# Attention output and state input of a hybrid decoder step as pairs of 64-column matmuls, and the weight sums spread anew

## The chip, the cores and the metric

The kernel runs on one core of a Trainium2 chip. The metric is the device time of one launch in microseconds, the median of the runs. A core has TensorE (PE, matmuls, its weight loads are listed as PEld), VectorE (DVE), ScalarE (ACT), GpSimd (POOL), and SyncE (SP), which here issues most DMAs.

## The reference

One decoder layer over 2064 prompt tokens (16 learned ones and 2048) and 8 x 4 sample tokens, model width 1024, FP32. A combined input projection feeds an attention group (8 heads of 64, 2 key/value heads, window of 128) and a state-space group (32 groups of 16 channels, 64 complex states each). Both outputs are normalised and projected together, and an MLP with squared ReLU follows. Cut to what the change touches:

```python
# attention of one block of 128 tokens: kk, vv are the block before and the block itself
logits = jnp.einsum('bnqkgd,bnskd->bnkgqs', qb, kk) * (HEAD_DIM ** -0.5)
p = sink_softmax(logits, mask, sink)
o = jnp.einsum('bnkgqs,bnskd->bnqkgd', p, vv)            # attention output
# state-space input of a group
bu_re = jnp.einsum('bsgh,gph->bsgp', ug, bbar_re)        # state input
bu_im = jnp.einsum('bsgh,gph->bsgp', ug, bbar_im)
# MLP
a = jnp.square(jax.nn.relu(jnp.einsum('bsd,df->bsf', hn, w_up)))
y = jnp.einsum('bsf,fd->bsd', a, w_down)
```

## The kernel before

The program runs in four stages. `phase_u` (to some 158 us) projects the state-space channels and prepares their matrices. `phase_att` (to 510 us) is the attention loop. `phase_mix` (to some 802 us) does the GLU of the state-space group and the output projection. `phase_mlp` does the MLP by a scheme of seven products in place of eight for 2 x 2 blocks, which needs sums and differences of blocks of the weights.

**The loop.** `tile_step(i)` handles one tile of 128 tokens and, beside it, one pair of state-space groups `pr = i + 1`. The order on TensorE, VectorE, ScalarE and GpSimd is that of the code for the first fifteen steps (`manual_schedule`); the last two steps and the other stages are ordered by a scheduler. In a step TensorE does the scores of heads (`scores`, L820), the q, k, v of the tile after next (`qkv`, L439 and L440), the transposes of the last tile's second half of probabilities (`ptrans`, L861), the second scores, the transposes of q and k (`tr`, L790 and L792), the state output (`s_out`, L942 and L946), the attention output of the last tile (`pv`, L873), the next state input (`s_in`, L908), and the transposes of this tile's first half of probabilities (L861 again). The probabilities of that half are scaled by VectorE on L852 (`normal`), the others by ScalarE on L854.

`pv` puts two heads on the two halves of 128 output partitions. The stationary tile `vr` holds 64 columns of v between zeros (192 columns), and a slice of 128 columns puts v left or right, so that four matmuls add up in one bank, of which two add zeros to each half. `s_in` does the same with `wz`, 64 columns of one group left and of the other right, with zeros between. `vr` and `wz` are filled with zeros once by GpSimd, and `s_load` loads `wz` by two DMAs a pair of groups. `s_out` uses the two row halves of the array instead: its stationary and moving slices are of 64 partitions each (L946). The two-bank pool `b2` holds one buffer, which `s_out`, `s_in` and the transposes of the projection share; `mm` has six banks.

**The weight sums.** `weight_sums` loads a block of 128 x 4 x 256 weights, does four subtractions (L1508, L1511, L1512, L1513) and stores the block. There are 64 blocks (32 for `w_up`, 32 for `w_down`). `sums_step` advances those under way and begins a new one, if the count is below `last`. Two steps a tile run in the loop on GpSimd (30 blocks), three a tile in the projection on VectorE up to block `SLAST = 44` (14 blocks), and one at every fourth step of the MLP's first product phase on VectorE (20 blocks). The store of a block waits in SP's queue for its sums.

**The projection.** For each tile `squares` adds squares on GpSimd (L1209, L1211), TensorE sums them over partitions (`norm_of`, L1216), VectorE scales (L1217) and GpSimd takes the power (L1218), which the evacuations of the projection's banks need (L1235 on ScalarE, L1340 on VectorE). `post_a` and `post_b` use GpSimd's power on L157. `turn` transposes the result two tiles later (L1363).

## Time and profile before

| | us |
|---|---|
| median of 3 runs (2098.76 to 2102.39) | 2098.87 |
| profiled execution | 2100.17 |
| its span, first to last instruction | 2098.4 |
| TensorE busy | 2037.1 (97%) |
| VectorE busy | 1591.9 (76%) |
| ScalarE busy | 1292.0 (62%) |
| GpSimd busy | 347.7 (17%) |
| share of the chain that ended last: TensorE | 82% |

Busy time is the sum of an engine's instructions. Matmuls are pipelined, so the start of the next line, not the end of a matmul, shows what a group takes. In the chain of waits each piece of time is put down to what the last instruction, followed back, waited for. A granted clock of 1.00 is 2.4 GHz on TensorE, 0.5 is 1.2 GHz. Spans on GpSimd are rough.

### The profile page before, as it was taken

To read this page: it belongs to the slowest core of one execution; us is meant where nothing else is said; L and a number is where in the kernel's file an instruction comes from. 1 tells how busy PE (TensorE), PEld (TensorE's weight loads), DVE (VectorE), ACT (ScalarE), POOL (GpSimd) and SP (SyncE) were. 2 spreads that over 40 slices of the span, in tenths; PEclk is the share of its full clock that TensorE was granted. 3 is DMA by queue.
4 is the path that set the end of the run, shared out by engine and by line. 5 is a ranking of instruction groups with operands and counts; after the bars stand their busy time and mean duration, and the time that the engine had idled before them with its cause. 6 is when DMAs were issued, how large, how long until landed. Compare 5 with 4: busy or idle time off the path is not lost.

```text
span 2098.4 us, 36246 instructions
## 1 busy us (share of the span) xinstructions
PE 2037.1 (97%) x12652; PEld 1915.3 (91%) x12652; DVE 1591.9 (76%) x3302; ACT 1292.0 (62%) x2787; POOL 347.7 (17%) x372
## 2 busy tenths in 40 slices
PE   7899999997999999999999999999999999999997
PEld 7877888876788879999999999999999999999996
DVE  8957888785867665898967866878668758787686
ACT  6644666666756556588655554886555547875555
POOL 5602444452424440000000000000000000000001
PEclk9999999998999999999999999999999999999999
DMA  8897778775686367888444655554445554444454
GB/s 297 239 212 211 195 201 203 203 183 137 212 270 212 118 203 231 277 276 281 143 143 136 194 184 140 164 167 138 136 141 186 172 152 136 154 142 140 136 164 147
DMA packets 360671, 387.10 MB, mean 184 GB/s; under 512 B 105208, under 2 KB 250264, under 8 KB 360472
## 3 DMA queue, kind: packets, MB, share of 16 engines
q1 hardware_dynamic: 293800, 378.14, 59.1%
q10 hardware_dynamic: 65792, 4.20, 2.2%
q0 software_dynamic: 896, 2.46, 0.4%
q8 instruction: 99, 1.62, 0.3%
q14 instruction: 84, 0.69, 0.1%
HBM read 303.26 MB, written 82.46 MB: 184 GB/s over the span
## 4 chain that ended last, share of the span: by engine, by line
PE 82%; DVE 7%; DMA 5%; ACT 2%; issue 2%; POOL 1%; SPq 1%; ACTq 0%; POOLq 0%; DVEq 0%
PE mm L111 22%; PE mm L112 22%; PE mm L113 22%; PE mm L439 4%; PE mm L873 2%; PE mm L440 2%; PE mm L820 1%; PE b L908 1%; PE mm L861 1%; DMA xr<-in_xT_dram 1%; PE b L946 1%; DVE U L1530 1%; PE b L1604 1%; PE b L942 1%; DMA UD<-U 1%
## 5 line engine op out<-in xcount | busy, mean ns | idle before, releaser
L111 PE MATMUL mm<-vh,wsh 128*128 128x352 f32 (+1 forms) x2624 | 838.2, 320 | 1.7 <-ACT wsh L96 1.7
L112 PE MATMUL mm<-vl,wsh 128*128 128x352 f32 (+1 forms) x2624 | 838.5, 320 | 0.0
L113 PE MATMUL mm<-vh,wsl 128*128 128x352 f32 (+1 forms) x2624 | 814.4, 320 | 0.0
L96 ACT ACTIVATE wsh<-wr 128x512 fp32r<-128x512 f32 x684 | 430.6, 630 | 440.9 <-PE mm L112 427.4
L97 DVE TENSOR_TENSOR wsl<-wr,wsh 128x512 fp32r<-128x512 f32 x684 | 472.4, 691 | 200.7 <-ACT wsh L96 198.5
L111 PEld LDWEIGHTS mm<-vh,wsh 128*128 128x128 f32 x2624 | 493.8, 188 | 2.2 <-ACT wsh L96 2.0
L112 PEld LDWEIGHTS mm<-vl,wsh 128*128 128x128 f32 x2624 | 493.1, 188 | 0.0
L113 PEld LDWEIGHTS mm<-vh,wsl 128*128 128x128 f32 x2624 | 488.0, 188 | 0.0
L157 POOL TENSOR_TENSOR yst<-yst,nhalf 128x1 f32<-128x1 f32 (+2 forms) x15 | 12.4, 826 | 1235.1 <-DVE yst L156 876.0
L1530 DVE TENSOR_TENSOR U<-U,mm 128x352 f32<-128x352 f32 (+3 forms) x240 | 140.1, 584 | 77.6 <-PE mm L113 76.9
L97 DVE TENSOR_TENSOR vl<-U,vh 128x352 fp32r<-128x352 f32 (+3 forms) x348 | 175.6, 506 | 1.5 <-ACT vh L96 1.0
L96 ACT ACTIVATE vh<-U 128x352 fp32r<-128x352 f32 (+3 forms) x348 | 162.9, 470 | 6.4 <-PE mm L112 6.2
L1563 ACT ACTIVATE U<-U 128x352 f32<-128x352 f32 (+1 forms) x192 | 92.6, 483 | 9.6 <-DVE U L1530 5.6
L1564 ACT ACTIVATE U<-U 128x352 f32<-128x352 f32 (+1 forms) x192 | 93.7, 489 | 4.2
L111 PE MATMUL mm<-xh,uwh 128*128 128x264 f32 (+1 forms) x256 | 73.3, 297 | 12.9 <-DVE U L531 7.0
L439 PE MATMUL mm<-qw,axh 128*128 128x512 f32 x224 | 85.0, 404 | 0.0
L112 PE MATMUL mm<-xl,uwh 128*128 128x264 f32 (+1 forms) x256 | 75.0, 296 | 0.0
L840 ACT ACTIVATE e<-e,mx 128x256 f32<-128x256 f32 x128 | 63.4, 497 | 16.5 <-DVE mx L834 16.5
L113 PE MATMUL mm<-xh,uwl 128*128 128x264 f32 (+1 forms) x256 | 72.9, 294 | 0.0
L863 ACT ACTIVATE PT<-mm 128x512 f32<-128x512 f32 x64 | 34.7, 595 | 56.1 <-PE mm L861 55.4
L97 POOL TENSOR_TENSOR axl<-axr,axh 128x1024 fp32r<-128x1024 f32 x14 | 34.6, 2472 | 169.3 <-ACT axh L96 128.8
L440 PE MATMUL mm<-qw,axh 128*128 128x256 f32 x224 | 62.6, 279 | 0.0
(372 smaller groups left out, 3567.4 us busy)
## 6 DMA issues: line engine op xcount, KB each, us to landing
wr<-TU SPq DMA_DIRECT2D x192, 256.0 KB
wr<-TD SPq DMA_DIRECT2D x192, 256.0 KB
wr<-in_w_down_dram SPq DMA_DIRECT2D x156, 256.0 KB
wr<-in_w_up_dram SPq DMA_DIRECT2D x144, 256.0 KB
wt<-in_w_up_dram SPq DMA_DIRECT2D x32, 512.0 KB
TU<-wt SPq DMA_DIRECT2D x32, 512.0 KB
Y<-in_w_down_dram SPq DMA_DIRECT2D x20, 512.0 KB
TD<-Y SPq DMA_DIRECT2D x20, 512.0 KB
```

Source lines behind the costliest of these rows:

```text
L96: ACT.activation(hi, src, AF.Copy)
L97: (eng or DVE).tensor_tensor(lo, src, r(hi), op=OP.subtract)
L111: PE.matmul(out, ah, bh, start=start, stop=False)
L112: PE.matmul(out, ah, bl, start=False, stop=False)
L113: LAST[0] = PE.matmul(out, al, bh, start=False, stop=stop)
L439: PE.matmul(pq[:n], lh(k), rh[k][:, 0:512], start=st, stop=sp_)
L440: PE.matmul(pkv[:n, :256], lh(k), rh[k][:, 512:768], start=st, stop=sp_)
L840: ACT.activation(e[:, j], e[:, j], AF.Exp, bias=mx[:, 1, j:j + 1], accum_out=mx[:, 3, j:j + 1])
L873: LAST[0] = PE.matmul(po[:, 256 * kv:256 * kv + 256], vr[:, sl[kb], kv, c0:c0 + 128], PT[u, kb][:, 256 * kv:256 * kv + 256], start=u == 0 ...
L1530: DVE.tensor_tensor(out, a, b, op=OP.add)
L1563: ACT.activation(x, x, AF.Relu)
L1564: ACT.activation(x, x, AF.Square)
```

## The change

`vr` and `wz` lose their zeros: the stationary operand is 64 columns, and the output goes to the lower or the upper 64 partitions of the bank, which is the left or the right column half of the array. In `pv` the loops over `kb` and `u` change places, so that the two halves alternate; each half adds up its own two matmuls. In `s_in` each matmul stands alone. The number of matmuls is the same. `s_load` loads `wz` by one DMA. The weight sums run one step a tile in the loop, two in every fifth (18 blocks); in the projection they run on GpSimd up to block 40 (22 blocks); in the MLP they begin at step 4 for step 12 and go to VectorE and GpSimd by turns (24 blocks).

```diff
--- before.py
+++ after.py
@@ -28,7 +28,7 @@
 MANUAL = {mybir.EngineType.PE, mybir.EngineType.DVE, mybir.EngineType.Activation, mybir.EngineType.Pool}
 WTB = 2
 WTM = 4
-SLAST = 44
+SLAST = 40
 SPT = 3
 WRB = 7
 WSB = 4
@@ -727,7 +727,7 @@
             ex = ExitStack()
             wx = pool(ex, "ax")
             kTr = [pw.tile([128, 4, 128], F32R, name=f"kT{n}") for n in range(2)]
-            vr = pw.tile([128, 4, 2, 192], F32, name="v")
+            vr = pw.tile([128, 4, 2, 64], F32, name="v")
             X, QK, QT, SM, PT, PO, TP = {0: X01[0], 1: X01[1]}, {}, {}, {}, {}, {}, {}
 
             def load_x(i):
@@ -771,7 +771,7 @@
             def v_in(i):
                 n = 128 if i < NT else NX
                 t = QK[i]
-                ACT.activation(vr[:n, slot(i), :, 64:128], t[:n, 10:12], AF.Copy)
+                ACT.activation(vr[:n, slot(i)], t[:n, 10:12], AF.Copy)
                 if i >= NT - 1:
                     v = t[:, 10:12].rearrange("p h d -> p (h d)")
                     if i < NT:
@@ -867,12 +867,10 @@
                     PO[i] = mm_bank()
                 po = PO[i]
                 sl = slots(i)
-                for u in range(2):
-                    c0 = 64 - 64 * u
-                    for kb in range(2):
-                        LAST[0] = PE.matmul(po[:, 256 * kv:256 * kv + 256], vr[:, sl[kb], kv, c0:c0 + 128],
-                                            PT[u, kb][:, 256 * kv:256 * kv + 256], start=u == 0 and kb == 0,
-                                            stop=u == 1 and kb == 1)
+                for kb in range(2):
+                    for u in range(2):
+                        LAST[0] = PE.matmul(po[64 * u:64 * u + 64, 256 * kv:256 * kv + 256], vr[:, sl[kb], kv],
+                                            PT[u, kb][:, 256 * kv:256 * kv + 256], start=kb == 0, stop=kb == 1)
                 if kv == 1:
                     at = wk.tile([128, 512], F32, name="at", tag="at", bufs=1)
                     ACT.activation(at.rearrange("p (k s c) -> p k c s", k=4, s=8),
@@ -882,7 +880,7 @@
 
 
             SX, SC, SS, SH = {}, {}, {}, {}
-            wz = [pw.tile([128, 2, 192], F32, name=f"wz{n}") for n in range(3)]
+            wz = [pw.tile([128, 2, 128], F32, name=f"wz{n}") for n in range(3)]
             hst = pw.tile([128, 2, NCY], F32, name="hst")
 
             def s_load(pr):
@@ -893,9 +891,7 @@
                     SP.dma_start(x[:, j], ap(UD, g * 16 * L8 * NC, [[NC, L8], [L8 * NC, 16], [1, NC]]))
                     SP.dma_start(kt[:, j], ap(KD, (pr // 4) * 32 * 960 + j * 16 * 960 + (pr % 4) * 240,
                                                   [[16, L8], [960, 16], [1, 128]]))
-                for n in range(2):
-                    SP.dma_start(wz[pr % 3][:, n].rearrange("p (j c) -> p j c", c=64)[:, 0:3:2],
-                                 BD[pr, :, 128 * n:128 * n + 128].rearrange("p (j c) -> p j c", c=64))
+                SP.dma_start(wz[pr % 3].rearrange("p n c -> p (n c)"), BD[pr, :, 0:256])
                 SP.dma_start(ct.rearrange("p a c -> p (a c)"), BD[pr, :, 256:512])
                 SP.dma_start(et.rearrange("p a c -> p (a c)"), ED[pr])
                 SC[pr] = (x, ct, kt, et)
@@ -905,7 +901,8 @@
                 pS = b2_bank()
                 for n in range(2):
                     for j in range(2):
-                        LAST[0] = PE.matmul(pS[:, n, :NC], w[:, n, 64 * j:64 * j + 128], x[:, j], start=j == 0, stop=j == 1)
+                        LAST[0] = PE.matmul(pS[64 * j:64 * j + 64, n, :NC], w[:, n, 64 * j:64 * j + 64], x[:, j],
+                                            start=True, stop=True)
                 SS[pr] = pS
 
             def s_rot(pr):
@@ -972,8 +969,6 @@
                 if pr + 3 < NPR:
                     s_load(pr + 3)
 
-            for n in range(3):
-                POOL.memset(wz[n], 0.0)
             s_load(0)
             load_x(2)
             for n in range(2):
@@ -1055,7 +1050,7 @@
                 if pr + 3 < NPR:
                     s_load(pr + 3)
                 if i < NT - 1:
-                    for _ in range(2):
+                    for _ in range(1 + (i % 5 == 2)):
                         sums_step(wk, POOL, WTB, 64, LAST[0])
                 if i == NT - 6:
                     glu_load()
@@ -1408,7 +1403,7 @@
                 load_a(ORD[n + 4])
             for _ in range(SPT):
                 if n < NT - 2:
-                    sums_step(gs, DVE, WTM, SLAST, LAST[0], 3)
+                    sums_step(gs, POOL, WTM, SLAST, LAST[0], 3)
             if n == NT - 2:
                 for x in SUMS:
                     advance(x, 6)
@@ -1675,8 +1670,8 @@
                     split_v(*steps[m + 2])
                 if m + 16 < len(steps) and steps[m + 16][1] == "u" and 8 <= u < 12:
                     split_v(*steps[m + 16][:3], u - 8)
-                if (b, ph) == (0, "u") and m >= 12 and m % 4 == 0:
-                    sums_step(None, DVE, 5, 64, LAST[0], 3)
+                if (b, ph) == (0, "u") and m >= 4 and m % 4 == 0:
+                    sums_step(None, (DVE, POOL)[NSUM[0] % 2], 5, 64, LAST[0], 3)
                 ahead(m)
                 if last(b, ph, p):
                     if c == 0 and u % 3 == 1 and u < 9:
```

TensorE in the loop, the end of one step: `s_out`, `pv` and `s_in` between the transposes of q (L792) and those of the probabilities (L861); `b` is the two-bank buffer, `sx` the moving input, and 64x256 is the output's size.

```order
 L790 MATMUL mm<-ident,qk 128x128
 L792 MATMUL mm<-ident,qk 128x128 x4
-L942 MATMUL b_3356<-sx,skt 128x268 x2
-L946 MATMUL b_3356<-hst,sc 128x268 x4
-L873 MATMUL mm<-PT,v 128x256 x8
-L908 MATMUL b_3390<-sx,wz_1998 128x276 x4
+L939 MATMUL b_3324<-sx,skt 128x268 x2
+L943 MATMUL b_3324<-hst,sc 128x268 x4
+L872 MATMUL mm<-PT,v 64x256 x8
+L904 MATMUL b_3358<-sx,wz_1998 64x276 x4
 L861 MATMUL mm<-ident,e 128x128 x8
 L820 MATMUL mm<-kT_1995,qTh 128x256 x2
```

The four groups stand where they stood, with outputs of 64 partitions in `pv` and `s_in`.

GpSimd in the projection, half a tile, before: `pq2` and `pq3` are the sums of squares, `pst` the column of powers.

```order
L1209 TENSOR_TENSOR pq2_6924<-pq_6922 128x256
L1218 TENSOR_TENSOR pst_6505<-pst_6505,nhalf_76 128x1
L157 TENSOR_TENSOR pst_6053<-pst_6053,nhalf_76 128x1
L1211 TENSOR_TENSOR pq3_6926<-pq2_6924 128x128
L1209 TENSOR_TENSOR pq2_6984<-pq_6981 128x256
L1218 TENSOR_TENSOR pst_6759<-pst_6759,nhalf_76 128x1
L157 TENSOR_TENSOR pst_6505<-pst_6505,nhalf_76 128x1
L1211 TENSOR_TENSOR pq3_6986<-pq2_6984 128x128
```

The same place in the change, where `wt` is a block of weights:

```order
L1204 TENSOR_TENSOR pq2_6821<-pq_6819 128x256
L1503 TENSOR_TENSOR wt_6588<-wt_6588 128x256
L1506 TENSOR_TENSOR wt_6588<-wt_6588 128x256
L1206 TENSOR_TENSOR pq3_6823<-pq2_6821 128x128
L1507 TENSOR_TENSOR wt_6588<-wt_6588 128x256
L1213 TENSOR_TENSOR pst_6656<-pst_6656,nhalf_76 128x1
L1204 TENSOR_TENSOR pq2_6881<-pq_6878 128x256
L157 TENSOR_TENSOR pst_6402<-pst_6402,nhalf_76 128x1
L1508 TENSOR_TENSOR wt_6588<-wt_6588 128x256
L1503 TENSOR_TENSOR wt_6595<-wt_6595 128x256
```

The sums stand between the sums of squares and the powers.

ScalarE at the start of the projection, before: `pah` is the split of an attention tile for the output projection, `zq` and `zh` belong to the input of the next GLU step.

```order
L96 ACTIVATE pah_6506<-pat_6251 128x512
L96 ACTIVATE pah_6609<-pat_6253 128x512
L1108 ACTIVATE zq_6024<-zu_6023 128x536
L1120 ACTIVATE zq_6024<-zq_6024 128x536
L1108 ACTIVATE zq_6029<-zu_6028 128x536
L96 ACTIVATE zh_6135<-zu_6023 128x536
L1120 ACTIVATE zq_6029<-zq_6029 128x536
L96 ACTIVATE zh_6141<-zu_6028 128x536
```

And the change, one GLU step later (the step above stands some twenty rows ahead, without a `pah` in it):

```order
L1103 ACTIVATE zq_6111<-zu_6110 128x536
L1115 ACTIVATE zq_6111<-zq_6111 128x536
L1103 ACTIVATE zq_6116<-zu_6115 128x536
L96 ACTIVATE pah_6403<-pat_6148 128x512
L96 ACTIVATE zh_6167<-zu_6110 128x536
L96 ACTIVATE pah_6506<-pat_6150 128x512
L1115 ACTIVATE zq_6116<-zq_6116 128x536
```

The two splits moved from ahead of the second GLU step's input to inside the third's.

## Rows read from the trace of the kernel before

**Rows 1.** Windows by stage: stretch, length, busy us by engine, clock, DMA share
```profile
core 0: us, PE busy (x) PEld busy (x) DVE busy (x) ACT busy (x) POOL busy (x), PEclk, DMA share, GB/s
209.00:434.00 225.00, 225.00 (x1423) 187.85 (x1419) 185.20 (x520) 139.46 (x374) 108.07 (x99) 1.00 0.78 197
434.00:510.00 76.00, 68.85 (x368) 54.53 (x366) 55.97 (x162) 51.19 (x133) 31.47 (x44) 0.93 0.59 153
510.00:570.00 60.00, 49.67 (x263) 42.73 (x264) 45.29 (x87) 42.29 (x88) 17.03 (x26) 0.91 0.67 197
570.00:712.00 142.00, 139.29 (x753) 118.84 (x753) 102.38 (x229) 81.79 (x180) 56.33 (x71) 0.98 0.65 216
802.00:1008.00 206.00, 204.28 (x1335) 203.96 (x1335) 167.13 (x338) 142.62 (x302) 0.00 (x0) 1.00 0.83 264
```

**Rows 2.** Chain of waits, 160 to 600 us: start, us, what
```profile
209.39 3.65 PE mm L873 x16
...
434.16 3.65 PE mm L873 x16
...
510.64 6.25 DMA ATD<-at
...
517.52 3.87 DMA pat<-ATD
```

**Rows 3.** TensorE's timeline, one tile of the loop: start, us, line, operation, count
```profile
370.68 1.07 PE L942 MATMUL b<-sx,skt 128*128 128x268 f32 x4
371.68 1.18 PE L946 MATMUL b<-hst,sc 64*128 64x268 f32 x8
372.79 3.72 PE L873 MATMUL mm<-PT,v 128*128 128x256 f32 x16
376.35 2.02 PE L908 MATMUL b<-sx,wz 128*128 128x276 f32 x8
378.20 1.04 PE L861 MATMUL mm<-ident,e 128*128 128x128 f32 x8
379.17 0.50 PE L820 MATMUL mm<-kT,qTh 64*128 64x256 f32 x4
```

**Rows 4.** TensorE's timeline, 54 to 57 us: 32 stationary columns
```profile
54.51 1.94 PE L398 MATMUL b<-ca,bd 128*32 128x128 f32 x16
```

**Rows 5.** VectorE's timeline, 350 to 392 us, in the loop
```profile
361.74 1.20 DVE L834 SCALAR_TENSOR_TENSOR mx<-mx,negsink 128x4 f32<-128x4 f32 x1
...
373.44 0.16 DVE L834 SCALAR_TENSOR_TENSOR mx<-mx,negsink 128x4 f32<-128x4 f32 x1
...
374.91 1.14 DVE L852 TENSOR_SCALAR e<-e,mx 128x256 f32<-128x256 f32 x4
```

**Rows 6.** GpSimd's timeline, in the loop and in the projection
```profile
360.52 2.41 POOL L97 TENSOR_TENSOR axl<-axr,axh 128x1024 fp32r<-128x1024 f32 x1 [10.14 <-DMA wz<-BD]
...
370.08 0.73 POOL L1513 TENSOR_TENSOR wt<-wt 128x256 f32<-128x256 f32 x1
...
571.44 1.60 POOL L1209 TENSOR_TENSOR pq<-pq 128x256 f32<-128x256 f32 x1
```

**Rows 7.** GpSimd groups, 209 to 434, then 570 to 712: busy, mean ns
```profile
L1508 POOL TENSOR_TENSOR wt<-wt 128x256 f32<-128x256 f32 x22 | 21.3, 968 | 0.0
...
L1209 POOL TENSOR_TENSOR pq<-pq 128x256 f32<-128x256 f32 x17 | 16.1, 947 | 6.1 <-ACT pq L1207 5.4
L1218 POOL TENSOR_TENSOR pst<-pst,nhalf 128x1 f32<-128x1 f32 x17 | 15.8, 932 | 13.0 <-DVE pst L1217 13.0
```

**Rows 8.** Line 1508, the sums' first operation, by form: ns min/median/max
```profile
L1508 POOL TENSOR_TENSOR wt<-wt x30: 719/751/1197, 199.4 to 504.3; 128x256 f32<-128x256 f32 x30
L1508 DVE TENSOR_TENSOR Y<-Y x20: 405/418/421, 833.2 to 977.5; 128x256 f32<-128x256 f32 x20
L1508 DVE TENSOR_TENSOR wt<-wt x14: 408/412/956, 564.6 to 643.6; 128x256 f32<-128x256 f32 x14
```

**Rows 9.** TensorE's timeline, 505 to 600 us: the wait at the projection's start
```profile
525.57 0.81 PE L111 MATMUL mm<-zh,gh 128*128 128x268 f32 x2 [6.04 <-ACT zh L96]
```

## The prediction

> **What bounds the kernel now.** I first read the windows by stage and then the chain of waits, and of the chain the attention loop, because the change edits TensorE's work there. From 209 to 434 us TensorE is busy in all of the time at the full clock, while VectorE is busy in 185 of 225 us and GpSimd in 108 [rows 1]. In the chain the sixteen matmuls of one tile's attention output (L873) return every 20.43 us ((434.16 - 209.39) / 11), so the loop lasts as long as TensorE's instructions, and no other engine ends a wait in it [rows 1, 2]. At 434 us the loop's tail begins (68.85 of 76 us busy), and at 510 us the projection, which starts with TensorE waiting (49.67 of 60 us busy) [rows 1]. From 570 us on TensorE is full again, and in the first part of the MLP it is busy in 204.28 of 206 us [rows 1]. The profiled execution took 2100.17 us for a span of 2098.4, so 1.8 us lie outside; the median of the runs, 2098.87, is 1.3 us lower, and I carry differences over to the median.
>
> **The change, part by part. The pairs.** One tile of the loop has 16 matmul instructions on L873 (8 in the program, two each on the engine, since the operands are FP32) and 8 on L908. They start at 372.79 and the next line starts at 378.20, which is 5.41 us [rows 3]. L908 alone takes (378.20 - 376.35) / 8 = 0.231 us an instruction of 276 columns, so one of 256 columns takes 0.2145. The change issues as many instructions, each with 64 stationary columns, in turns for the left and the right half of the array. What two such matmuls take when the halves differ no row shows. The nearest row is L946: the same type in turns on the two row halves. Its 8 instructions take 372.79 - 371.68 = 1.11 us [rows 3], and 8 one after the other would take 8 x 0.231 x 268/276 = 1.79, four pairs 0.90. So row halves run at the same time there, and 0.21 us is left over. L942 ahead of it (four full instructions, 0.90, in 1.00 us) leaves 0.10, and L873 behind it (16 x 0.2145 = 3.43, in 3.56) leaves 0.13; together 0.44 us for going into row halves and out again, 0.22 us a change of the array's division. One thing is not in that row: row halves read one moving operand each from 64 partitions, while column halves both read all 128. The upper bound is therefore no overlap at all: 0.231 each as now. A matmul with few columns costs no more than its moving columns: L398 with 32 stationary columns does 16 in 1.94 us, 0.12 each for 128 columns, and its weight loads are hidden [rows 4]. The lower bound is half. I take half, since L946 has the same data type, the same alternation and the same engine: 8 x 0.2145 + 4 x 0.231 = 2.64 us, and one change of division more (row halves to column halves to full, where it was row halves to full), 0.22. So a tile's 5.41 us, 0.13 of them at the boundary that stays, become 2.64 + 0.13 + 0.22 = 2.99, and 2.42 us are saved.
>
> The Trainium skill speaks on both sides. TensorEngine Tiling (Array Packing), Key Properties, says that changing the tiling mode drains the engine; the 0.44 us above agree. TensorE: Matmul & The Clock Gate, Measured speedup vs the span model, gives 2.38 times for three column tiles; by that ratio two would give about 1.6, an estimate, and a tile would save 1.7 us, not 2.4. No run here shows it.
>
> **What is late next.** The eight transposes L861 follow L908 and take the probabilities that VectorE scales on L852. Those four end at 374.91 + 1.14 = 376.05 [rows 5]. That time hangs on the tile's earlier transposes and on ScalarE, which the change doesn't touch. L861 would start at 378.20 - 2.42 = 375.78, and its fourth transpose, three steps of (379.17 - 378.20) / 8 = 0.12 us later [rows 3], needs the fourth piece just after it is written. I put 0.15 us a tile for that (none, if the pieces come in time; 0.4 with a late signal). Net 2.27 us a tile. VectorE is not the next bound: its load was 16.8 us a tile, and it falls. While GpSimd's sums run, from 360.5 to 370.8, L834 takes 1.20 us, and after them 0.16 [rows 5, 6]; with half the sums, half of that goes. It costs nothing now and gives nothing beyond this.
>
> The Trainium skill, SBUF — State Buffer, Who interferes with whom, says that a VectorE instruction with two SBUF inputs contends with a GpSimd instruction that reads SBUF. L834 has two, and its 1.20 beside 0.16 us agree. The rule speaks against the sums' new place in the projection; its price there is in the third rival.
>
> The twelve tiles between the rows of 209.39 and 434.16 give 12 x 2.27 = 27 us [rows 2]. The four attention outputs of the tail would give 9.7 more if TensorE were the bound there, but it is busy in 69 of 76 us, and the rest waits; I take 4 (0 to 10). The two first states ahead of the loop give 1. The merged load of the stationary tile (one DMA for two), the smaller fills with zero and the narrower copy of v lie beside TensorE's work and are costed at nothing; the loop has 0.78 DMA share now and loses 0.8 of 2 MB of sums a tile [rows 1].
>
> **The weight sums.** Of 64, the loop keeps 18 of 30 on GpSimd, the projection gets 22 on GpSimd for 14 on VectorE, and the MLP 24, by turns, for 20 on VectorE. VectorE loses 14 x 4 x 0.412 = 23 us in the projection and, with 12 for 20, 8 x 4 x 0.418 = 13 us in the MLP [rows 8]; TensorE is full in both, so that buys little: what TensorE lacks from 570 to 712 us is 2.7 us. GpSimd gets 22 x 4 = 88 instructions, by the order all between the points that lie at 570 and 712 us now. There it works 56 us [rows 1], on the sums of squares, which TensorE's norm waits for, and on the powers, which the evacuations of the projection's banks wait for [rows 7]. At the typical 0.75 us [rows 8] the load becomes 56 + 66 = 122 of 142 us, at the loop's mean of 0.968 [rows 7] it becomes 141. So cover is there, but thin: 15 half tiles lie in the stretch by the order, 142 / 15 = 9.5 us each, a norm's operand is made up to two of them ahead (its tile has two buffers), and six banks let an evacuation be about one late. I charge 5 us (0 to 15). In the MLP GpSimd is idle [rows 1], the sums come at the same pace (every fourth step) and only start eight steps earlier: nothing, up to 2 us for later weights.
>
> **The projection's start.** ScalarE there splits two attention tiles (L96 pah) ahead of the next GLU input, and they wait for a DMA out and back in, 510.64 to 521.39 [rows 2]; TensorE sits idle for 6.04 us at 525.57 [rows 9]. In the changed order these splits stand behind that input. I credit 4 us (0 to 8).
>
> **The sum.** -27 - 4 - 1 + 5 - 4 = -31 us, so 2069 for the profiled execution and **2068 us** for the median. Its own range is 2051 (all sixteen tiles at 2.42, the first states' 1, the start's 8, no charge for GpSimd: 2098.87 - 38.7 - 1 - 8) to 2087 (0.4 us of wait a tile, 2 in the tail, nothing at the start, 15 for GpSimd: 2098.87 - 24.2 - 1 - 2 + 15).
>
> **The rivals.**
> 1. *The pairs overlap only in part*, or another chain takes half the gain: 1.2 us a tile, -15 in the loop and tail, so 2083 with the other terms near zero. For it speaks that L861 would arrive within 0.3 us of L852 already. Chance 0.10.
> 2. *The column halves don't overlap.* Then each tile pays the change of division: 16 x 0.22 = +3.5, +5 for GpSimd, -4 at the start, -1 in the tail: 2102. For it speaks the doubled reading of the moving operand, against it L946. Chance 0.14.
> 3. *GpSimd bounds the projection: slower.* The 88 instructions wait for VectorE's two-input work, as VectorE does for them. The excess is 56 + 88p - 142 us at price p. At 0.968 it is none. At 1.6 us, which single rows of a 128x256 sum show [rows 6], it is 55, and the time 2068 - 5 + 55 = 2118. The kernel is slower than before from 36 us of excess on, p = 1.4. Against it speaks the mean of 0.947 of the same-sized sums (L1209) in the projection itself [rows 7]. Chance 0.08.
>
> **How the numbers follow.** The forecast has 0.68. The range has to leave out no more than 2 in 10: from 2051, the end of the forecast's own, to 2100, which takes in rival 1 and the fast edges of 2 and 3 (0.65 + 0.10 + 0.06). Faster by over 0.2% (4.2 us, about what a measurement of this kernel can tell from no change) is nearly all of the forecast, rival 1 and the mild third: 0.79. Within it falls most of rival 2: 0.08. Slower are the rest of 2 and most of 3: 0.13.
>
> **What would show it.** The period of a tile in the chain should be 18.2 us for 20.43, the new attention output about 2.0 us and the new state input about 1.1 to 1.2 up to the transposes; at 3.6 and 1.9 the halves don't overlap. TensorE's waits in the loop should name L861 and VectorE and stay below 0.4 us a tile. In the projection GpSimd should be busy above 0.8 from the first to the last sum, and TensorE should wait for its sums of squares for less than 15 us. The forecast is wrong if the period stays above 19.5 us, or if the stretch from the last attention output to the MLP's first matmul grows by over 15 us.

## The result, and the profile after

The changed kernel takes 2076.78 us (median of 4 runs, 2074.60 to 2077.88) beside 2100.05 us of the kernel before; the ratio is 0.9887, its 95% interval 0.9870 to 0.9904. That is 23 us less, where the forecast was 31 less (2068 us). The profiled execution took 2076.74 us for a span of 2075.0, against the 2098.4 of before, so 23.4 us are to be found in the trace.

From the page of the changed kernel, the chain of work that ended last, by engine:

```profile
PE 81%; DVE 7%; DMA 4%; POOL 3%; ACT 3%; issue 2%; SPq 0%; ACTq 0%; POOLq 0%; DVEq 0%
```

TensorE still holds most of the chain, and it is busy in 96% of the span. New is GpSimd's share, 3% of the chain where it was 1%: some engine waits for it now. Where, the windows by stage tell (stretch, length, busy us of each engine with its count, granted clock, DMA share, GB/s); the first line is the loop, the second the tail, the others are the projection from 539 to 690 us.

```profile
core 0: us, PE busy (x) PEld busy (x) DVE busy (x) ACT busy (x) POOL busy (x), PEclk, DMA share, GB/s
207.00:425.00 218.00, 217.19 (x1549) 169.86 (x1548) 199.52 (x561) 147.57 (x407) 85.96 (x72) 1.00 0.73 179
425.00:481.00 56.00, 38.74 (x226) 28.33 (x223) 41.19 (x123) 41.95 (x106) 16.85 (x25) 0.82 0.43 101
...
539.00:594.00 55.00, 54.31 (x307) 46.29 (x305) 38.48 (x69) 29.81 (x65) 43.45 (x59) 1.00 0.89 292
594.00:658.00 64.00, 59.52 (x314) 50.32 (x312) 46.30 (x69) 34.85 (x74) 59.17 (x71) 0.92 0.83 277
658.00:690.00 32.00, 30.04 (x150) 24.47 (x150) 23.17 (x45) 18.74 (x42) 18.10 (x25) 1.00 0.51 168
```

Two lines stand out beside [rows 1]. In the tail TensorE is busy in 39 of 56 us. The tail of [rows 1], 69 of 76, begins a tile earlier; over the same stretch of work, from the thirteenth to the last attention output, TensorE was busy in 47.9 of 54.6 us (454.6 to 509.2) and is now in 42.4 of 59.7 (425.5 to 485.2). So this stretch got longer by 5 us, although its matmuls got shorter. And from 594 to 658 us, in the middle of the projection, it is busy in 59.5 of 64 us at a clock of 0.92, while GpSimd is busy in 59: in the kernel before, its counterpart from 626 to 682 us has TensorE busy in 55.7 of 56 us at full clock.

To find the 23.4 us I cut both traces at the same eight points, seven of them instructions of TensorE, and compare the lengths between the cuts. The cuts are: the first attention output; the end of the last state output (L946, now L943); the projection's first matmul on the GLU output; the second and the fourth transposes of the state attention (L1287, now L1282); the MLP's first matmul; its first transposes (L1604, now L1599); the end. The table has all kernels of this study, in us. "Tile" is the time from the first to the thirteenth attention output, divided by twelve.

| kernel | start | loop, to the last state output | to the GLU output | to the 2nd transposes | to the 4th | to the MLP | its first part | rest | tile |
|---|---|---|---|---|---|---|---|---|---|
| before | 209.3 | 263.4 | 69.5 | 84.3 | 82.5 | 79.3 | 361.6 | 948.5 | 20.43 |
| changed | 207.2 | 237.3 | 66.6 | 83.6 | 92.9 | 79.3 | 359.6 | 948.5 | 18.20 |
| changed, second time | 205.4 | 238.3 | 67.8 | 83.5 | 92.5 | 79.3 | 359.6 | 948.5 | 18.18 |
| pairs_alone | 207.8 | 250.1 | 66.6 | 86.9 | 82.5 | 79.3 | 361.0 | 948.4 | 18.83 |
| sums_alone | 209.4 | 261.7 | 68.5 | 80.9 | 92.6 | 79.3 | 359.6 | 948.5 | 20.43 |
| half_then_half | 209.5 | 244.0 | 66.7 | 82.0 | 92.3 | 79.3 | 359.6 | 948.2 | 18.79 |
| proj_dve | 207.0 | 237.5 | 66.5 | 85.6 | 88.9 | 79.4 | 359.6 | 948.2 | 18.20 |
| gp14 | 209.5 | 237.2 | 66.7 | 84.0 | 89.5 | 79.3 | 366.5 | 949.0 | 18.19 |
| dve14 | 208.3 | 237.3 | 66.9 | 85.9 | 82.5 | 79.3 | 365.5 | 949.8 | 18.19 |
| tail_norm | 206.1 | 238.5 | 68.8 | 83.2 | 93.0 | 79.3 | 359.6 | 949.0 | 18.21 |
| tail_z | 207.1 | 238.4 | 67.7 | 84.9 | 92.8 | 79.3 | 359.6 | 948.4 | 18.19 |
| best_a | 207.7 | 239.6 | 67.4 | 85.9 | 82.4 | 79.3 | 359.6 | 948.0 | 18.37 |
| best_b | 206.0 | 240.2 | 66.6 | 87.0 | 82.3 | 79.3 | 359.6 | 949.7 | 18.51 |

From before to changed: -2.1 at the start, -26.1 in the loop, -2.9 up to the GLU output, -0.7 up to the second transposes, **+10.4 up to the fourth**, 0, -2.0 in the MLP's first part, 0: together -23.4. So the loop gave what it should, and this stretch of the projection took ten back. The -2.1 at the start can't be put down to the change: in six later runs of this table the code up to there is that of the changed kernel, and their starts lie between 205.4 and 209.5 us.

The loop first. TensorE's timeline of one tile (start, us, line, operation, shapes, count), to be laid beside [rows 3]:

```profile
351.59 1.17 PE L943 MATMUL b<-hst,sc 64*128 64x268 f32 x8
352.70 1.95 PE L872 MATMUL mm<-PT,v 128*64 128x256 f32 x16
354.47 1.10 PE L904 MATMUL b<-sx,wz 128*64 128x276 f32 x8
355.50 1.27 PE L861 MATMUL mm<-ident,e 128*128 128x128 f32 x8
356.71 0.50 PE L820 MATMUL mm<-kT,qTh 64*128 64x256 f32 x4
```

From L872's first to L861's first it is 355.50 - 352.70 = 2.80 us, where it was 5.41. Sixteen instructions last 354.47 - 352.70 = 1.77 us: eight pairs at 0.2145 are 1.72. The two column halves work at the same time, all of it. The transposes L861 then take 356.71 - 355.50 = 1.21 us for 0.97: 0.24 us more, and the waits below name VectorE's scaling for it.

Now the ten microseconds. GpSimd's timeline in the projection (start, us, line, operation, count; in brackets idle time and who ended it), from the place where the loss begins:

```profile
593.56 4.29 POOL L1503 TENSOR_TENSOR wt<-wt 128x256 f32<-128x256 f32 x3
597.82 0.92 POOL L1204 TENSOR_TENSOR pq<-pq 128x256 f32<-128x256 f32 x1
598.70 2.96 POOL L1506 TENSOR_TENSOR wt<-wt 128x256 f32<-128x256 f32 x3
601.62 3.29 POOL L1507 TENSOR_TENSOR wt<-wt 128x256 f32<-128x256 f32 x3
604.86 0.93 POOL L1206 TENSOR_TENSOR pq<-pq 128x128 f32<-128x128 f32 x1
605.75 0.55 POOL L157 TENSOR_TENSOR pst<-pst,nhalf 128x1 f32<-128x1 f32 x1
606.27 0.55 POOL L1213 TENSOR_TENSOR pst<-pst,nhalf 128x1 f32<-128x1 f32 x1
606.79 2.62 POOL L1508 TENSOR_TENSOR wt<-wt 128x256 f32<-128x256 f32 x3
```

There is no idle time in it. The sums come three at a time, and the small steps that others need (the squares' sums L1204 and L1206, the norm's power L1213) stand between them: the two halves of one sum of squares, L1204 at 597.82 and L1206 at 604.86, are 7 us apart. Who waits for the power, from 545 to 712 us (waiting instruction, what it waited for, us in all, times, longest; before, it was 10.9 us in four waits):

```profile
ACT po L1230 <- POOL pst L1213: 16.2, 6, 5.4
```

and on SyncE's queue, which issues the transfers in order, from 552 to 712 us:

```profile
SPq L1510 <- POOL wt L1508: 32.0, 15, 10.5
```

L1510 is the write of a finished sum back to memory. While it waits for GpSimd's last step, every load behind it in the queue waits too. What TensorE makes of all this shows in windows of 4 us:

```profile
620.00:624.00 4.00, 4.00 (x19) 3.14 (x18) 3.62 (x7) 3.89 (x9) 3.79 (x6) 1.00 1.10 385
624.00:628.00 4.00, 2.44 (x11) 1.50 (x10) 1.72 (x5) 1.39 (x4) 4.00 (x8) 0.80 1.09 373
628.00:632.00 4.00, 1.08 (x3) 0.89 (x4) 3.96 (x5) 2.34 (x4) 4.00 (x3) 0.50 0.73 278
632.00:636.00 4.00, 4.00 (x11) 3.13 (x10) 1.79 (x7) 0.79 (x3) 3.92 (x7) 0.50 0.73 252
636.00:640.00 4.00, 4.00 (x18) 3.22 (x18) 2.71 (x7) 2.71 (x7) 3.66 (x6) 0.92 1.08 350
```

It idles for 4.5 us from 624 to 632, and its granted clock falls to 0.50 (the lower level, 1.2 GHz) until about 637: 4 us then hold 11 matmuls where they held 19. Of the 8 us by which the stretch from 594 to 658 is longer than its counterpart of before, 4.2 are idle time and the other 3.8 go with the lower clock; the rest of the ten comes after 658 us, where TensorE idles for 2 us more.

The longest idle piece, 3.36 us, shows which small step it was. TensorE waits for an evacuation L1230, and on ScalarE that one stands behind a square L1202, which waits for GpSimd's L1204 because the tile `pq` has one buffer (TensorE's timeline, then ScalarE's):

```profile
630.92 0.80 PE L111 MATMUL mm<-oh,psh 128*128 128x512 f32 x1 [3.36 <-ACT po L1230]
```

```profile
629.66 0.63 ACT L1202 ACTIVATE pq<-pat 128x512 f32<-128x512 f32 x1 [4.27 <-POOL pq L1204]
```

So here it is the sum of squares that came late on GpSimd, not the power, which had ended at 626.8 us. The DMA share is 1.05 to 1.10 from 612 to 628 us, so the DMA engines are full at the same time.

### The profile page after: what moved, and what is told of

It reads as the page before. It is cut to its first block, busy times and chain, and to the rows that moved or that the text cites. A ratio compares the mean times of both kernels' runs of the same rounds, so it can differ in the third digit from the quotient of the medians.

```text
span 2075.0 us, 36204 instructions
## 1 busy us (share of the span) xinstructions
PE 1999.3 (96%) x12652; PEld 1866.5 (90%) x12652; DVE 1590.7 (77%) x3214; ACT 1292.3 (62%) x2787; POOL 428.0 (21%) x457
## 4 chain that ended last, share of the span: by engine, by line
PE 81%; DVE 7%; DMA 4%; POOL 3%; ACT 3%; issue 2%; SPq 0%; ACTq 0%; POOLq 0%; DVEq 0%
PE mm L111 23%; PE mm L112 23%; PE mm L113 23%; PE mm L439 4%; PE mm L440 2%; PE mm L861 1%; PE mm L820 1%; PE mm L872 1%; DMA qwr<-in_w_in_dram 1%; DMA pat<-ATD 1%; PE b L1599 1%; POOL wt L1503 1%; POOL wt L1507 1%; DVE xl L97 1%; DVE e L831 1%
## 5 line engine op out<-in xcount | busy, mean ns | idle before, releaser
L97 DVE TENSOR_TENSOR wsl<-wr,wsh 128x512 fp32r<-128x512 f32 x684 | 477.8, 699 | 194.0 <-ACT wsh L96 191.6
L1558 ACT ACTIVATE U<-U 128x352 f32<-128x352 f32 (+1 forms) x192 | 92.8, 485 | 14.4 <-DVE U L1525 9.9
L840 ACT ACTIVATE e<-e,mx 128x256 f32<-128x256 f32 x128 | 63.4, 498 | 18.6 <-DVE mx L834 18.5
L111 PE MATMUL mm<-oh,psh 128*128 128x512 f32 (+1 forms) x136 | 57.0, 419 | 7.1 <-ACT po L1230 3.4
```

Source lines behind the costliest of these rows:

```text
L97: (eng or DVE).tensor_tensor(lo, src, r(hi), op=OP.subtract)
L111: PE.matmul(out, ah, bh, start=start, stop=False)
L840: ACT.activation(e[:, j], e[:, j], AF.Exp, bias=mx[:, 1, j:j + 1], accum_out=mx[:, 3, j:j + 1])
L1558: ACT.activation(x, x, AF.Relu)
```

## The experiments

Each is timed against the kernel before on the same chip; the lengths are in the table above.

### The two parts apart

pairs_alone takes the changed kernel and puts the sums back:

```
-SLAST = 40
+SLAST = 44
-                    for _ in range(1 + (i % 5 == 2)):
+                    for _ in range(2):
-                    sums_step(gs, POOL, WTM, SLAST, LAST[0], 3)
+                    sums_step(gs, DVE, WTM, SLAST, LAST[0], 3)
-                if (b, ph) == (0, "u") and m >= 4 and m % 4 == 0:
-                    sums_step(None, (DVE, POOL)[NSUM[0] % 2], 5, 64, LAST[0], 3)
+                if (b, ph) == (0, "u") and m >= 12 and m % 4 == 0:
+                    sums_step(None, DVE, 5, 64, LAST[0], 3)
```

> Only the 64-column pairs; the weight sums stay as in the kernel before (two a tile on GpSimd in the loop, 14 on VectorE in the projection, 20 on VectorE in the MLP). Theory: the pairs give the loop its gain, and the sums on GpSimd cost about 10 us in the projection. In the changed kernel a tile takes 18.06 us where one sum runs beside it and 18.6 to 18.9 where two do; with two in every tile the period should be 18.6 to 18.9, which gives 12 x (20.43 - 18.75) = 20 us in the loop, 2 ahead of it, some 2 between the loop and the projection as in the changed kernel, and no loss in the projection: 2074 us (2070 to 2079). Rival: the loop's gain needs fewer sums beside it, and the period stays above 19.4 us: 2084 or more. Second rival: the loss in the projection is not GpSimd's; then it is here as well, and the time is 2084 too, but with a period below 18.9.

sums_alone is the kernel before with the same four places the other way round.

> Only the new distribution of the weight sums; the attention output and the state input keep the 128-column matrices filled with zeros. Theory: the loop is bound by TensorE and stays at 20.43 us a tile, GpSimd's sums in the projection make TensorE wait and lose about 10 us there, and the MLP gains about 2: 2107 us (2103 to 2111). Rival: the sums beside the loop cost it time; then the loop gets faster with 18 of 30, and the time is 2098 or less. Second rival: GpSimd's sums only hurt when the projection comes earlier or in another order, as in the changed kernel: then 2097 to 2100.

Measured: pairs_alone 2086.11 us, ratio 0.9934 (0.9918 to 0.9950); sums_alone 2106.09 us, ratio 1.0024 (1.0015 to 1.0034). The pairs by themselves gain 15 us, the sums by themselves lose 5 (the traced execution of sums_alone, 2102.39 us, was the fastest of its ten), and together they gain 23: **the two parts need each other**. In the loop sums_alone has the same 20.43 us a tile, so fewer sums give nothing there as long as TensorE's own instructions set the period. With the pairs they decide: two sums in every tile make the period 18.07 us at first, 18.5 to 18.8 in the middle and 19.2 to 19.3 in the last four, 18.83 in the mean, and the loop up to the last state output takes 12.8 us more than in the changed kernel. TensorE's waits and those of its weight loads from 207 to 425 us say for whom, in pairs_alone

```profile
PEld mm L861 <- DVE e L852: 11.4, 12, 1.4
...
PE mm L861 <- DVE e L852: 5.6, 11, 0.9
```

and in the changed kernel

```profile
PEld mm L861 <- DVE e L852: 6.0, 12, 0.9
...
PE mm L861 <- DVE e L852: 0.8, 3, 0.4
```

So by the waits VectorE is the next bound behind the pairs. Its instructions' durations (they overlap in part) add up to 19.9 us a tile in pairs_alone and to 19.4 in the changed kernel, over the same twelve tiles; L834 of [rows 5] is not the one that grows, it is shorter with two sums (0.35 us in the mean, 0.84 in the changed kernel). The mean period is the one I had expected; that the time is 12 us above the expected 2074 has its largest piece at the loop's end, where TensorE waits once for ScalarE's copy of the last state output and ScalarE for an attention tile from memory. TensorE's and ScalarE's timelines there:

```profile
441.10 2.11 PE L904 MATMUL b<-sx,wz 128*64 128x276 f32 x8 [5.47 <-ACT sy L945]
```

```profile
437.70 0.63 ACT L96 ACTIVATE pah<-pat 128x512 fp32r<-128x512 f32 x1 [5.93 <-DMA pat<-ATD]
```

With two sums a tile ahead of it in the same queue that load came late; in the changed kernel TensorE's wait at this place is 0.3 us. The projection is the other half of the proof: pairs_alone, with 14 sums on VectorE there, takes the 82.5 us of before from the second to the fourth transposes; sums_alone, without any pairs, takes 92.6. The ten microseconds belong to the sums. But a part of them is only moved: up to the second transposes pairs_alone takes 86.9 us and the changed kernel 83.6, so from the GLU output to the fourth transposes the sums' new place costs 7.1 us (176.5 for 169.4).

### Do the pairs need their turns?

```
-                for kb in range(2):
-                    for u in range(2):
-                        LAST[0] = PE.matmul(po[64 * u:64 * u + 64, 256 * kv:256 * kv + 256], vr[:, sl[kb], kv],
...
+                if kv == 1:
+                    for u in range(2):
+                        for g in range(2):
+                            for kb in range(2):
+                                LAST[0] = PE.matmul(po[64 * u:64 * u + 64, 256 * g:256 * g + 256], vr[:, sl[kb], g],
```

> The changed kernel, but the eight attention output matmuls of a tile go first all to the left column half and then all to the right one, not in turns; the state input stays in turns. The number of stationary columns, of instructions and of loads is the same. Theory: the gain comes from two halves at work at the same time, and needs the turns: the sixteen instructions take 3.4 to 3.6 us for 1.9, a tile 19.6 to 19.8 us, and the time is 2077 + 16 x 1.6 = 2103 us (2096 to 2106). Rival: the gain comes from the narrower stationary matrix itself (half the columns to load and to drive): 1.9 us and 2077 stay. Second rival: the engine looks ahead over several instructions and overlaps the two blocks in part: 2.4 to 3.0 us, 2085 to 2095.

Measured: 2081.38 us, ratio 0.9906 (0.9888 to 0.9924), 18.79 us a tile. The theory had 2103, so it fell, and the second rival holds in its mechanism (2.86 us for the sixteen, forecast 2.4 to 3.0); its time, 2085 to 2095, was too high. TensorE's timeline of one tile:

```profile
359.89 2.21 PE L874 MATMUL mm<-PT,v 128*64 128x256 f32 x13
361.73 0.45 PE L905 MATMUL b<-sx,wz 128*64 128x276 f32 x1
361.94 0.38 PE L874 MATMUL mm<-PT,v 128*64 128x256 f32 x1
362.01 0.40 PE L905 MATMUL b<-sx,wz 128*64 128x276 f32 x1
362.15 0.38 PE L874 MATMUL mm<-PT,v 128*64 128x256 f32 x1
362.24 0.40 PE L905 MATMUL b<-sx,wz 128*64 128x276 f32 x1
362.37 0.38 PE L874 MATMUL mm<-PT,v 128*64 128x256 f32 x1
362.48 1.20 PE L905 MATMUL b<-sx,wz 128*64 128x276 f32 x5
363.61 1.09 PE L861 MATMUL mm<-ident,e 128*128 128x128 f32 x8
```

The state input's matmuls for the left half (L905) start while the attention output's last three for the right half (L874) are still to start: the instructions of the two halves overtake each other. In the same way the first of the right half starts 0.92 us after the first of the left one, with the left's fifth, and not after its eighth. Both lines together take 363.61 - 359.89 = 3.72 us, against 2.80 in turns, and 16 x 0.2145 + 0.93 = 4.36 if the sixteen ran one after the other. Of the two orders turns are the better one, but some look-ahead does part of it without: by these starts, an instruction passed three that stood ahead of it for the other half.

### Which engine, and how many sums in the projection

The changed kernel does 22 sums in the projection on GpSimd; the one before did 14 on VectorE. Three runs fill in the other cells. proj_dve moves the 22 to VectorE:

```
-                    sums_step(gs, POOL, WTM, SLAST, LAST[0], 3)
+                    sums_step(gs, DVE, WTM, SLAST, LAST[0], 3)
```

> The changed kernel, with the 22 sums of the projection on VectorE in place of GpSimd. Theory: in the changed kernel GpSimd's queue is full from 592 to 636 us, its small power steps for the norm stand behind the sums, the evacuations wait for them and TensorE for the banks; it waits some 7 us and then runs some 10 us at half clock: about 10 us in all. On VectorE the sums take 22 x 4 x 0.41 = 36 us of an engine that is busy in 70 to 75% there; TensorE's waits between 560 and 690 us fall below 3 us, and the time is 2068 us (2065 to 2072). Rival: VectorE takes GpSimd's place as the late engine, since the evacuations need it too: waits of TensorE for VectorE of 6 us or more there, and 2074 or more.

gp14 does 14 there, on GpSimd, and dve14 14 on VectorE (with the edit of proj_dve too); both leave 32 to the MLP:

```
-SLAST = 40
+SLAST = 32
-                if (b, ph) == (0, "u") and m >= 4 and m % 4 == 0:
+                if (b, ph) == (0, "u") and m >= 4 and m % 3 == 1:
```

> The changed kernel with 14 weight sums in the projection in place of 22, on GpSimd as in the change; the MLP takes the other 32, every third step in place of every fourth, by turns as in the change. Theory A: what costs 10 us in the projection is the number of sums, by way of the DMA queue and the 22 MB that they move; 14 cost nothing in the kernel before, so 2067 us (2064 to 2071) and no loss between the second and the fourth transposes of the state attention. Theory B: GpSimd's queue, in which the norm's small steps stand behind three sums at a time, costs it whatever the number; then some 6 of the 10 us remain, 2072 to 2075, with waits of ScalarE's evacuations for the power steps (L1213) of 6 us or more between 552 and 690 us. Rival: the MLP pays for 32 sums what the projection gains: 2077, with the loss between the MLP's start and its first transposes.

> As the last one, with the 14 sums of the projection on VectorE, as in the kernel before. In the run with 22 sums on VectorE the profile lost 6.4 us in one place, where the next GLU input waited 7.4 us for its DMA behind the sums' DMAs. Theory A (number and DMA): no loss, as in the kernel before, 2067 us (2064 to 2071), within 2 us of the run with 14 on GpSimd. Theory B (GpSimd's queue): 2067 here too, but 5 us or more less than with 14 on GpSimd. Rival: the same DMA wait in the same place, 2073 or more.

Measured: proj_dve 2077.62 us, ratio 0.9893 (0.9875 to 0.9912); gp14 2080.69, 0.9909 (0.9891 to 0.9927); dve14 2075.08, 0.9876 (0.9854 to 0.9899). None is the 2067 or 2068 that I had expected, and the lengths say why. From the second to the fourth transposes, in us:

| | on VectorE | on GpSimd |
|---|---|---|
| 14 sums | 82.5 (dve14, before: 82.5) | 89.5 (gp14) |
| 22 sums | 88.9 (proj_dve) | 92.9 (changed) |

Either step alone costs 6.4 to 7 us here, both 10.4. The stretch ahead of it gives some back when the sums are on GpSimd: with both stretches the four cells are 168.4 (dve14), 173.5 (gp14), 174.5 (proj_dve) and 176.5 (changed), so the steps cost 5.1 and 6.1, both 8.1. There are two mechanisms; that each costs time the table shows, how it does so is read from the rows. On GpSimd it is the queue, and in gp14 the DMA share is 0.58 from 597 to 658 us, so there the DMA engines are not full. ScalarE's evacuations L1230 wait for the power 16.2 us in the changed kernel (above) and, from 545 to 712 us, in gp14 and in dve14

```profile
ACT po L1230 <- POOL pst L1213: 18.3, 7, 5.4
```

```profile
ACT po L1230 <- POOL pst L1213: 10.1, 5, 4.2
```

With 22 on VectorE it is the transfers. The windows of the stretch, of proj_dve and of dve14, differ in the DMA share, 0.96 to 0.64:

```profile
596.00:652.00 56.00, 55.72 (x312) 47.91 (x311) 48.56 (x110) 32.18 (x69) 26.48 (x27) 1.00 0.96 320
```

```profile
598.00:654.00 56.00, 55.72 (x314) 47.95 (x313) 41.91 (x87) 36.45 (x77) 23.95 (x28) 1.00 0.64 210
```

and behind them comes the next GLU input. Its load in the chain of waits (start, us), in proj_dve and in dve14:

```profile
644.55 7.42 DMA zu<-YD
```

```profile
643.92 3.96 DMA zu<-YD
```

ScalarE and VectorE then make that input for TensorE, which in proj_dve is busy in 28.9 of 33.5 us from 652 us on. Its waits there name VectorE, 6.9 us from 560 to 700 us (1.1 in dve14), which is the sign of proj_dve's rival. The chain leads from them back to the load, but VectorE is busier too (48.6 for 41.9 of 56 us), and no run separates the two. In the changed kernel both hold: the chain goes through GpSimd's sums at first, and the same load takes 6.82 us at 656.38.

dve14 and gp14 do not gain what they get back, for the MLP's first part grew by 5.9 and 6.9 us over the changed kernel's. Its window from 790 to 970 us, of dve14 and of the changed kernel:

```profile
790.00:970.00 180.00, 177.47 (x1137) 175.38 (x1137) 160.08 (x284) 122.35 (x258) 57.84 (x60) 0.99 0.98 333
```

```profile
790.00:970.00 180.00, 180.00 (x1176) 180.00 (x1176) 150.92 (x274) 126.95 (x263) 50.02 (x48) 1.00 0.91 300
```

With 32 sums at every third step the DMA engines are full (0.98), with 24 at every fourth not quite (0.91). VectorE is busier as well (160 for 151 us), and TensorE's waits name it and ScalarE, which split the weights; whether the weights or VectorE came late isn't separated. So in gp14 both theory B (7.0 us of the ten stay) and the rival (the MLP pays) hold, and in dve14 theory A holds for the projection, which loses nothing, but the MLP pays there too.

### The tail

In the changed kernel TensorE waits in the tail mostly for one line, the last normalization on ScalarE (420 to 560 us):

```profile
PE mm L861 <- ACT e L854: 13.7, 3, 7.4
PE mm L111 <- ACT zh L96: 6.2, 1, 6.2
```

The tail is not in the order of the program; a scheduler sets it, and with the pairs it put eight weight splits (L99, 5.0 us on ScalarE) ahead of tile 14's four L854, where before the splits had stood behind. tail_norm puts these back ahead:

```
-                if i:
+                if i and i != NT - 1:
                     rden(i - 1, 1)
                     normal(i - 1, 1)
...
                 if i == NT - 2:
+                    rden(i, 1)
+                    normal(i, 1)
                     for k in range(4):
                         w_out(k)
```

> The changed kernel, but the last normalization of tile 14 (four activations L854 on ScalarE, and the two steps on VectorE ahead of them) is written at the end of tile 14, ahead of the eight splits of the output weights (L99), where the scheduler had put it in the kernel before; in the changed kernel it stands behind them. Theory: the tail lost 9 us against the forecast because ScalarE does 5.6 us of weight splits while TensorE waits for these four activations (7.4 us in one piece at 448 to 456 us, with half clock after it). With the order of before the wait shrinks below 2.5 us, the waits for L854 in the tail from 13.7 to 5 to 7 us, and the time is 2070 us (2066 to 2073). Rival: the tail hangs on VectorE's chain (maximum, sums, scaling) and the wait only changes its name: 2075 to 2078.

Measured: 2080.40 us, ratio 0.9903 (0.9885 to 0.9921). Not better than the changed kernel, as the rival had it. The waits of the same stretch:

```profile
PE mm L111 <- ACT zh L96: 9.7, 3, 8.7
PE mm L861 <- ACT e L854: 6.2, 3, 2.9
```

The wait for L854 fell by 7.5 us, as the theory had it, and the last attention output came 4.6 us earlier (1.1 of them from the start); but TensorE then waited longer for the GLU's input, and from the last state output to the GLU output it took 68.8 us for 66.6 and 67.8 in the changed kernel's two runs. The tail's attention can get shorter without the tail's end getting nearer. tail_z tries that end, by writing the first two GLU inputs ahead of the last tile's second half:

```
+                if i == NT - 1:
+                    z_a(0)
+                    z_b(0)
+                    z_a(1)
                 if i < NT:
                     scores(i, 1)
...
                     w_out_load(5)
-                    z_a(0)
-                    z_b(0)
-                    z_a(1)
```

> The changed kernel, but the first two GLU inputs are written one half tile earlier, ahead of the last tile's second half of scores. From the end of the last state output to the projection's first matmul on the GLU output all runs so far took 66.4 to 69.6 us, with tails of quite different waits. Theory: that stretch is the chain of the GLU inputs (load, four steps on ScalarE and VectorE each, in turns with the tail's own work on the same engines); with the inputs earlier in ScalarE's order it shrinks by 3 us or more, to below 64 us, and the time is 2073 or less. Rival: the chain is held by the load of the input or by the attention tiles, and the stretch stays above 66 us: 2076 to 2080.

Measured: 2078.20 us, ratio 0.9890 (0.9873 to 0.9907), and the stretch is 67.7 us. Rival again. Its chain of waits shows what stands in between:

```profile
495.03 8.03 DMA pat<-ATD
...
503.62 0.63 ACT zh L96
504.25 0.33 ACT pah L96
```

The attention tiles of the projection come back from memory only at 503 us, after the last attention output (its last matmul starts at 487.5), and their splits (pah) and the next GLU inputs (zh) share ScalarE at 503 us. In all rows of the table this stretch took 66.5 to 69.5 us, with tails of quite different waits. Which of the two holds it isn't settled.

### A version from these findings

best_a spreads the sums by the table: 22 in the loop (two in every second tile), 14 on VectorE in the projection, 28 in the MLP at every fourth step. best_b puts 26 in the loop (two in three of four tiles) and 24 in the MLP.

```
-SLAST = 40
+SLAST = 36
-                    for _ in range(1 + (i % 5 == 2)):
+                    for _ in range(1 + (i % 2 == 1)):
-                    sums_step(gs, POOL, WTM, SLAST, LAST[0], 3)
+                    sums_step(gs, DVE, WTM, SLAST, LAST[0], 3)
```

(best_b: SLAST stays 40, and the loop has `i % 4 != 0`.)

> The changed kernel with the sums spread by what the runs so far showed: the loop does two sums in every second tile (22 in all, for 18), the projection 14 on VectorE, the MLP 28 at every fourth step by turns. Theory: 14 on VectorE cost the projection nothing (10 us back), a tile with two sums costs 0.55 us (4 more: 2 us lost), and 28 sums at the pace of every fourth step don't fill the DMA engines in the MLP as 32 at every third step did (5 us lost there): about 1 us lost. Together 2077 - 10 + 2 + 1 = 2070 us (2067 to 2073). Rival: tiles with two sums in every second place build up a backlog on GpSimd and VectorE, as with two in each (periods up to 19.3 us), or the MLP loses as with 32: 2074 or more.

> As the last one, with 26 sums in the loop (two in three of four tiles), 14 on VectorE in the projection and 24 in the MLP. Theory: eight more tiles with two sums than in the changed kernel cost 8 x 0.55 = 4.4 us, the projection gives 10 back, the MLP stays as in the changed kernel: 2071 us (2068 to 2074). Rival: with so many the period grows from tile to tile as it did with 30 (18.7 to 19.3 us): 2074 to 2078.

Measured: best_a 2070.73 us, ratio 0.9855 (0.9839 to 0.9871); best_b 2072.19, 0.9859 (0.9839 to 0.9879). Both came out within 1.2 us of the expectation, in part by luck: the projection has its 82.4 us back, the MLP keeps 359.6 (the expectation of best_a had 1 us lost there), and the loop pays 2.3 and 2.9 (4.4 expected for best_b); but the stretch up to the second transposes takes 85.9 and 87.1 us for 83.6, which no term had. To be sure of 6 us, best_a and the changed kernel ran once more, side by side:

> The changed kernel as it is, a second time, on the same chip and beside the same runs of the kernel before as the next one, so that the two can be compared: 2077 us, ratio 0.989 (0.988 to 0.990). Its stretch from the second to the fourth transposes of the state attention should again lose 10 to 11 us against the kernel before.

> The version with 22 sums in the loop, 14 on VectorE in the projection and 28 in the MLP a second time. Theory: it keeps its 6 us against the changed kernel: 2071 us, ratio 0.9855, with an interval that leaves the changed kernel's ratio out. Rival: the 6 us were the spread between calls, and the two differ by less than 3 us.

Measured: the changed kernel 2077.50 us (2074.80 to 2079.16), ratio 0.9888 (0.9871 to 0.9904), best_a 2070.64 us (2069.62 to 2071.46), ratio 0.9855 (0.9840 to 0.9870). No run of the one reaches into those of the other: best_a beats both kernels, the changed one by 6.9 us: the stretch between the transposes gives 10, and the loop and the way up to that stretch take some 4 of them.

## Why the prediction was right or wrong

**The pairs: right, in size too.** The step "a tile's 5.41 us become 2.99" measured 2.80; the wait of L861 for VectorE, put at 0.15, measured 0.24; the net gain of 2.27 a tile is (379.17 - 372.79) - (356.71 - 352.70) = 2.37 by [rows 3] and the rows above. The period came out as 18.07 in tiles with one sum and 18.6 to 18.9 in those with two, 18.20 in the mean, for 18.2 forecast. Over twelve tiles that is 26.9 us, for the 27 of the sum. (The two rows that the prediction names for the twelve tiles are eleven apart; the trace has twelve of 20.43, so the 27 stands.) The 1 us ahead of the loop can't be told from the spread of the starts, 4 us. What was off within it: the extra change of the array's division, priced at 0.22, is hardly there. Sixteen instructions leave 1.77 - 1.72 = 0.05 us over and the next eight 1.03 - 4 x 0.231 = 0.11, where one boundary left 0.13 before; and L943 ahead of them leaves the same 0.21 as L946 did. Going from row halves to column halves cost what going from row halves to the full array had cost.

The Trainium skill, TensorEngine Tiling (Array Packing), Key Properties, says that a change of the mode drains the engine; the trace shows that in 0.21 us in front of L872, and less, 0.11 us, between column halves and the full array. The Trainium skill, TensorE: Matmul & The Clock Gate, Measured speedup vs the span model, has 2.38 times for three column tiles, from which I had estimated 1.6 for two; here two ran at a full factor of two, 0.2145 us a pair as for one.

**"VectorE is not the next bound", "costs nothing now and gives nothing beyond this": wrong in its reason.** The sum had no term for the relief in the loop, and needed none, since both parts were there together. But pairs_alone shows that the relief carries 12.8 us of the loop's 26, some 7.6 of them by the period, 18.83 us a tile and up to 19.3 with VectorE as the bound, and 5 by the late tile at the loop's end. The step that failed is the comparison of VectorE's busy time (16.8 us a tile) with the period: what counts is when L852 ends in the tile, and that moves with what GpSimd does beside it. L834, the row by which the prediction judged that, was not what grew.

**The tail and the projection's start, "4 (0 to 10)" and "4 (0 to 8)": too high.** From the thirteenth attention output to the GLU output 2.1 us came and in the following stretch 0.7, 2.8 in all for 8. In the tail TensorE is not the bound, as said, and the pairs' 9.7 us there went into waits of 13.7 us for L854 (3.2 before) and the lower clock after them (0.83 from 425.5 to 485.2 us, 0.91 over the same work before). The credit at the start came true for the second GLU step, which TensorE now begins without a wait (at 490.1 us), but the wait of 6.04 us [rows 9] came back at the third, where the splits stand now:

```profile
502.38 0.82 PE L111 MATMUL mm<-zh,gh 128*128 128x268 f32 x2 [6.20 <-ACT zh L96]
```

That input had been ready on VectorE at 497.6 us. ScalarE splits it for TensorE only at 501.70, behind a step that waited 3.43 us for the load of a later input (zu) and behind a split of an attention tile. So the step that failed is that the order of the splits removes the wait; it moved it by one GLU step. The other is the adding up: I credited the tail and the start apart, though the GLU's inputs set the end of both. tail_norm and tail_z moved waits about in it and the end stayed.

**GpSimd in the projection, "+5 (0 to 15)": the mechanism half right, the size too small.** It cost 10.4 us in the stretch, and 10.1 in sums_alone, without the pairs; with the stretch before counted in, 8.1 against dve14. The term of 5 was half of the one and three fifths of the other; its range held. The price of an instruction was near where the rows had put it (0.75 to 0.97): of the four steps 0.80, 0.91, 0.91 and 1.06 us in the mean from 539 to 700 us, so the load stayed below the time that there was, and the third rival's point (p = 1.4 us) was far. GpSimd was busy in 121 of 151 us, 0.80, at the edge of what I had said; TensorE's waits stayed below 15 us. The step that failed is the comparison of a load with a stretch: the sums come three at a time and hold an engine that works in order, so what comes late are the small steps behind them, the power and the sum of squares, not GpSimd as a whole. And a part was not in it at all: that the sums' write-backs wait on SyncE's queue (32.0 us for GpSimd, in fifteen waits) and that 22 sums move 22 MB for 14, at a DMA share of 0.83 to 0.96. I had named SyncE's queue for nothing but the stationary tile. In that stretch the number alone costs 6.4 us on VectorE, the engine alone 7.0.

**The MLP, "nothing, up to 2 us": 2.0 us faster.** TensorE's one wait for ScalarE's weight split in the first part of before (1.7 us) is gone. sums_alone has the same 359.6 us and pairs_alone 361.0, so it goes with the sums; whether by eight sums fewer on VectorE or by the earlier begin isn't separated. dve14 shows that the cover has an edge: at 32 sums it is gone.

**Sum.** In the loop -26.9 for -27, ahead of it -2.1 for -1, in the tail and at the projection's start -2.8 for -8, between the transposes +10.4 for +5, in the MLP -2.0 for 0: the miss of 7.6 us is 5.2 in the tail and start and 5.4 in the projection, 0.1 in the loop, less 2.0 in the MLP and 1.1 ahead of the loop. In part that is luck: two misses of 10.6 us go the same way, and 3 us from elsewhere offset them.

**The rivals.** Partial overlap and no overlap are out by the timeline of one tile. Of the third, the place was right and the price far too high. The share that it was given as "slower" went by a mean load; what it does in the projection is neither the rival's 55 us nor the charge's 5.

## What to carry to other kernels

Two matmuls with 64 stationary columns each on the two column halves, in turns, took the time of one here (0.2145 us a pair), and such pairs are to be looked for wherever a stationary matrix is filled up with zeros. Behind such a gain ask at once which engine now ends the wait, and test the change's other parts with it and without: here one part cost 5 us alone and gained 9 beside the other. Work moved to an idle engine is to be priced by its longest burst in front of a small step that others wait for, and by every transfer that it issues into a shared queue, not by the engine's mean load.

## What the runs showed of the hardware that I had not expected

Matmuls for one column half start ahead of earlier ones for the other: in half_then_half the first of the right half starts with the fifth of the left (0.92 us behind the first), and the sixteen take 2.86 us from first start to the last one's end, for 1.95 in turns and 3.72 as 128-column matmuls [rows 3]. Going into column halves from row halves cost the 0.21 us that leaving row halves had cost anyway.

Around 4.5 us without work between 624 and 632 us of the changed kernel, TensorE's clock stood at the lower level for some 10 us (the windows of 4 us above). The stretch lost 3.8 us by that, nearly as much as by the waits themselves.
